# A two-layer decoder trunk on one core: table transfers with 64 rows outermost, ring slots by use, taps tile by tile

## The chip, the cores and the metric

The kernel runs on one core of a Trainium2 chip. Five engines take part, each with its own instruction stream: TensorE (PE, matmuls; PEld is its loading of weights), VectorE (DVE), ScalarE (ACT), GpSimd (POOL) and SyncE (SP), which here issues every transfer between the chip's main memory (DRAM) and the core's working memory (SBUF), one after the other. The transfers themselves are carried out by 16 DMA engines of the core. The metric is the device time of one execution in microseconds (us); the median of three runs is compared.

## The reference

The input x is 1024 tokens by 1024 channels, all float32. Two layers follow each other, each with an RMSNorm before and after its mixer and a residual.

```python
# layer 0: dilated attention, 16 heads of 64, three groups (window, dilation) = (128,1), (512,4), (2048,16)
proj = h @ w_in                                   # 1024 x (9*1024 + 1024): q, k, v of three groups, and a gate z
for g: o_g, lse_g = dilated_group_attention(q_g, k_g, v_g, rel_bias, window, dilation)
o = sum_g softmax_g(lse)[g] * o_g
x = x + rms_norm((o * silu(z)) @ w_out)
# layer 1: 64 groups of 16 channels, 64 complex states each
u, z = split(h @ w_in)                            # 1024 x 2048
a_bar = exp(A*dt); b_bar = (a_bar - 1)/A * B
states = scan over tokens of  s <- a_bar*s + b_bar u
y = real(C states) + d*u
g = gelu(y); y = g * sigmoid(g @ w_glu + b_glu)
x = x + rms_norm((y * silu(z)) @ w_out)
```

## The kernel before

Every large product is made as three products of a high and a low part (hi*hi, hi*lo, lo*hi), so each weight tile of 128 channels is loaded as float32 (`wraw`, L95, two buffers), cast by ACT to its high part (`whi`, L83), and the remainder is taken by DVE or POOL (`wlo`, L84). One such tile takes 48 matmuls of 128x512, 24 for each half of the tokens (`psj`, L110).

The program runs in this order. First the **value phase** (`v_phase`, up to about 390 us): the values of attention are computed chunk by chunk with a seven-product scheme (`Quads.values` and `Quads.quad`, matmuls L394 into `psq`). Each chunk loads its raw weights (`v<-in_w_v_dram`, L381) and stores its results to DRAM (`v_dr`, L400). Between these products the tables that layer 1 needs are built for its eight tiles `et` of eight groups each (`Prep.powers` and `Prep.products`): DVE forms `ca` (powers of the state's decay times C) and `zr`, `zi` (the same with B); `ca` goes to DRAM as `ca_dr` (L1208, two transfers a tile); PE forms the convolution taps from `ca` and `bd` (`pk`, L1223), which go through `Ks` to `k_dr` (L1228); PE turns `z` (`ptb`, L1235), which goes through `BT` to `bt_dr` (L1237).

Then comes **attention**, eight pairs of heads by three groups (about 390 to 1290 us). POOL makes one table of rotations per pair and group (`rt`, L1280 to L1285), which is stored as `rot_dr` (L1288, 24 transfers). The output of a pair goes to `on_dr`, and merging weights are read back as `mw`. The output product of layer 0 (`pso`, L865 to L867) runs until about 1390 us.

**Layer 1** (`layer1`, about 1390 to 1665 us) multiplies sixteen weight tiles, eight for u and eight for z. I call them w0 to w15 in order of use; w0 and w1 are loaded during the output product of layer 0. Between them run the stages of each tile `et`: `ssm_loads` reads the tables back (`BT`, `Cg` and `Sg` from `rot_dr`, `CA`, and the taps `M`), `ssm_input` reads the tile's u (`U`, L1333, which was stored by `u_dr`, L1400), `ssm_states` runs `pv` (L1348) and the scan on DVE, and `ssm_outputs` runs `py` (L1375) and stores y. The stages of tiles 0 and 1 are loaded ahead of everything. After that come the gated product (`glu`) and the output.

Small staging tiles come from a ring with two tags, "a" with three buffers and "b" with four. `Ctx.slot` gives the tags in turn unless a tag is named. A framework (a tile scheduler) orders the instructions on each engine: within the program's dependences it places them by a simulated timeline and by priorities, and the loads of weights have a high priority. What is written earlier in the program is therefore not always issued earlier, and a change of one transfer can move others. Each engine then runs its list strictly in order. SP is such a list too: a transfer that SP can't hand over holds all that stand behind it.

Of the kernel before, what the change touches and what calls it, by code (L numbers as in the profile page):

```python
# [15 lines left out]
F32 = mybir.dt.float32  # L16
# [7 lines left out]
P = 128  # L24
S = 1024
# [20 lines left out]
HEADS = (slice(0, 64), slice(64, 128))  # L46
# [218 lines left out]
class Quads:  # L265
# [47 lines left out]
    def quad(self, raw, order, product, banks, use):  # L313
# [3 lines left out]
        c, nc = self.c, self.c.nc  # L317
        b11, b12, b21, b22 = raw
        n = b11.shape[2]
# [27 lines left out]
        for i in order:  # L347
# [8 lines left out]
            with c.tc.high_priority(AHEAD):  # L356
                for b, ps in enumerate(acc):
# [3 lines left out]
                    elif i == 1:  # L361
                        t = c.slot("c11")
# [774 lines left out]
class Prep:  # L1137
# [60 lines left out]
    def powers(self, et):  # L1198


        c, nc = self.c, self.c.nc
# [4 lines left out]
        for n in range(2):  # L1206
            dst = bass.AP(c.ca_dr.tensor, c.ca_dr.offset + (et * 2 + n) * 64 * 1152, [[144, 2], [1152, 64], [288, 4], [1, 144]])
            nc.sync.dma_start(dst, ca[n])  # L1208
        z = outers(c, [c.slot("zr"), c.slot("zi")], self.tmp, [y[:, ps] for y in self.bp], [raw[:, n, :, 0] for n in range(2)])
# [5 lines left out]
    def products(self, et):  # L1215
# [8 lines left out]
        Ks = c.slot("Ks")[0:32].rearrange("p (k x) -> p k x", k=4)  # L1224
# [5 lines left out]
        for b in range(2):  # L1230
            BT = c.slot("BT").rearrange("p (g r s) -> p r g s", g=4, r=2)
# [28 lines left out]
def rotations(c, et, part):  # L1260
# [26 lines left out]
    dst = bass.AP(c.rot_dr.tensor, c.rot_dr.offset + (et * 3 + part) * 64 * S, [[P, 2], [S, 64], [256, 4], [1, P]])  # L1287
    nc.sync.dma_start(dst, out.rearrange("p (k x) -> p k x", k=4))  # L1288
# [14 lines left out]
def ssm_loads(self):  # L1303
# [9 lines left out]
    if et % 4 == 0:  # L1313

        c.taps = c.pb.tile([P, 4, 8, P], F32, tag=("b1", "b3")[et // 4], name="taps")
        koff = c.k_dr.offset + et * 8 * 16 * 240
        for m in range(8):
            src = bass.AP(c.k_dr.tensor, koff + 16 * m, [[240, 16], [16 * 240, 32], [1, 128]])
            nc.sync.dma_start(c.taps[16 * m:16 * m + 16].rearrange("p e g x -> p (e g) x"), src)
    self.M = c.taps[:, et % 4]  # L1320
    dr = c.rot_dr
    nc.sync.dma_start(self.BT, c.bt_dr[et].rearrange("p (g x) -> p g x", g=8))
    nc.sync.dma_start(self.Cg.rearrange("p g x -> p (g x)"),
                      bass.AP(dr.tensor, dr.offset + et * 3 * 64 * S, [[0, 2], [S, 64], [1, S]]))
    nc.sync.dma_start(self.Sg.rearrange("p g x -> p (g x)"),
                      bass.AP(dr.tensor, dr.offset + (et * 3 + 1) * 64 * S, [[S, P], [1, S]]))
    nc.sync.dma_start(self.CA, c.ca_dr[et].rearrange("p (g x) -> p g x", g=8))

# [62 lines left out]
def layer1(c, a, h1, ws):  # L1391
# [17 lines left out]
    groups = [Ssm(c, a, e) for e in range(8)]  # L1409
    at = [[] for _ in range(40)]  # L1410
# [209 lines left out]
```

## Time and profile before

| | |
|---|---|
| three runs, median | 1868.26 us (1868.19 to 1870.78) |
| the profiled execution, its own time | 1870.87 us |
| its span, first to last instruction | 1869.1 us |
| PE busy | 1707.9 us (91%) |
| DVE, ACT, POOL busy | 1045.7, 798.3, 461.7 us |
| mean granted PE clock | 0.963 |
| moved by the DMA engines | 212.67 MB, 114 GB/s mean |

Times in a row are microseconds from the start of the span unless they are marked ns. A row of the timeline gives start, duration, engine, line of the source, operation, output<-input with shapes, how often, and in brackets the idle time of that engine just before, with what ended it. SPq rows are the transfers that SP issues; a duration well above a third of a microsecond there means that SP was held while it handed the transfer over. A row of the windows gives a stretch, its length, the busy time of each engine in it with the number of instructions, the granted PE clock, the mean busy share of the 16 DMA engines and the GB/s that they moved. A row of the waits gives who waited, for whom, us in total, times, longest.

### The profile page before, as it was taken

How to read it: one execution, taken by the hardware profiler on the slowest of the kernel's cores; microseconds unless marked ns; L12 is line 12 of the kernel's file. 1: busy time of each engine (PE TensorE's matmuls, PEld its weight loads, DVE VectorE, ACT ScalarE, POOL GpSimd, SP SyncE). 2: the span in 40 equal slices, each digit the busy share in tenths (PEclk: the TensorE clock that was granted, in tenths of full speed). 3: DMA queues.
4: the chain of work that ended last, by engine and by line, in shares of the span. 5: the costliest groups of instructions: out<-in, count | busy, mean ns of one | idle time of the engine just before them, and what ended most of it. 6: DMA issues, size and time to landing. Idle time of an engine off the chain costs nothing. (4 is left out here: it accounts for less than half of the span.)

```text
span 1869.1 us, 25668 instructions
## 1 busy us (share of the span) xinstructions
PE 1707.9 (91%) x9262; PEld 1436.9 (77%) x9262; DVE 1045.7 (56%) x2565; ACT 798.3 (43%) x1912; POOL 461.7 (25%) x314
## 2 busy tenths in 40 slices
PE   7999978899979989899999999998995499989998
PEld 5889867787868778687787888876885488877886
DVE  7788766624544545455454555557461278764532
ACT  5222221235645656456465656564351122233411
POOL 2000000031242232322425142314220044432221
PEclk9999989899989999899999999998998799999999
DMA  6223342351231222313223232417257756646432
GB/s 237 70 67 104 113 139 88 116 161 50 72 93 47 74 78 82 84 57 98 68 74 105 75 106 82 127 58 198 91 126 154 179 187 216 197 130 192 146 119 90
DMA packets 174691, 212.67 MB, mean 114 GB/s; under 512 B 35153, under 2 KB 131172, under 8 KB 174564
## 3 DMA queue, kind: packets, MB, share of 16 engines
q1 hardware_dynamic: 174564, 211.03, 38.4%
q8 instruction: 73, 1.20, 0.3%
q14 instruction: 54, 0.44, 0.1%
HBM read 154.03 MB, written 56.96 MB: 113 GB/s over the span
## 5 line engine op out<-in xcount | busy, mean ns | idle before, releaser
L110 PE MATMUL psj<-hh,whi 128*128 128x512 f32 x896 | 363.9, 406 | 15.8 <-DVE ql L201 6.6
L110 PE MATMUL psj<-hl,whi 128*128 128x512 f32 x896 | 362.2, 404 | 0.0
L110 PE MATMUL psj<-hh,wlo 128*128 128x512 f32 x896 | 360.9, 403 | 0.0
L84 POOL TENSOR_TENSOR wlo<-wraw,whi 128x1024 fp32r<-128x1024 f32 x48 | 115.3, 2401 | 427.1 <-ACT whi L83 414.5
L110 PEld LDWEIGHTS psj<-hh,whi 128*128 128x128 f32 x896 | 172.2, 192 | 53.3 <-ACT kh L214 8.1
L110 PEld LDWEIGHTS psj<-hh,wlo 128*128 128x128 f32 x896 | 171.9, 192 | 35.9 <-issue 0.3
L110 PEld LDWEIGHTS psj<-hl,whi 128*128 128x128 f32 x896 | 172.4, 192 | 34.6 <-issue 0.7
L509 ACT ACTIVATE lg<-lg,nm 128x128 f32<-128x128 f32 (+1 forms) x384 | 168.2, 440 | 34.0 <-DVE nm L504 33.4
L498 DVE CUSTOM_DVE_ANT_0 lg<-psl,T 128x128 f32<-128x128 f32 (+1 forms) x384 | 116.7, 347 | 98.1 <-PE psl L495 97.0
L110 PE MATMUL psj<-h1h,whi 128*128 128x512 f32 (+1 forms) x272 | 108.8, 400 | 49.9 <-ACT whi L83 27.9
L83 ACT CAST whi<-wraw 128x1024 fp32r<-128x1024 f32 x80 | 83.6, 1045 | 165.5 <-PE psj L110 94.2
L394 PE MATMUL psq<-whi,v 128*128 128x256 f32 x640 | 122.1, 287 | 5.4 <-DVE v L366 5.4
L84 DVE TENSOR_TENSOR kl<-psj,kh 64x512 fp32r<-64x512 f32 x96 | 66.0, 687 | 86.6 <-ACT kh L83 85.3
L394 PEld LDWEIGHTS psq<-whi,v 128*128 128x128 f32 x640 | 101.8, 192 | 7.1 <-DVE v L366 6.1
L110 PE MATMUL psj<-h1l,whi 128*128 128x512 f32 (+1 forms) x272 | 107.0, 393 | 0.2 <-DVE h1l L84 0.2
L110 PE MATMUL psj<-h1h,wlo 128*128 128x512 f32 (+1 forms) x272 | 105.9, 391 | 0.0
L84 DVE TENSOR_TENSOR ph<-pt,ph 128x512 fp32r<-128x512 f32 (+1 forms) x128 | 78.8, 620 | 42.3 <-ACT ph L83 40.8
L110 PEld LDWEIGHTS psj<-h1h,whi 128*128 128x128 f32 x272 | 53.0, 195 | 62.4 <-ACT whi L83 28.4
L394 PE MATMUL psq<-wlo,v 128*128 128x256 f32 x320 | 91.8, 288 | 3.0 <-DVE wlo L84 3.0
L84 DVE TENSOR_TENSOR wlo<-wraw,whi 128x1024 fp32r<-128x1024 f32 x32 | 40.0, 1253 | 95.3 <-ACT whi L83 94.2
L83 ACT CAST whi<-v 128x1024 fp32r<-128x1024 f32 x35 | 36.8, 1051 | 128.1 <-PE psq L394 101.2
L1227 POOL TENSOR_TENSOR Ks<-Ks,O 32x64 f32<-32x64 f32 x8 | 3.8, 478 | 337.4 <-ACT Ks L1225 320.1
(292 smaller groups left out, 4055.2 us busy)
## 6 DMA issues: line engine op xcount, KB each, us to landing
wraw<-in_w_in_dram SPq DMA_DIRECT2D x56, 512.0 KB
mw<-wt_dr SPq DMA_DIRECT2D x48, 256.0 KB
v<-in_w_v_dram SPq DMA_DIRECT2D x20, 512.0 KB
vp<-v_dr SPq DMA_DIRECT2D x16, 512.0 KB
wraw<-in_ssm_w_in_dram SPq DMA_DIRECT2D x16, 512.0 KB
v_dr<-v SPq DMA_DIRECT2D x30, 256.0 KB
rot_dr<-rt SPq DMA_DIRECT2D x24, 256.0 KB
ca_dr<-ca SPq DMA_DIRECT2D x16, 288.0 KB
```

The source lines that it names most:

```text
L83: nc.scalar.copy(hi, src)
L84: return (engine or nc.vector).tensor_tensor(lo, src, f32(hi), op=ALU.subtract)
L110: nc.tensor.matmul(ps, a[:, s], b[:, k, :], start=first and k == 0 and n == 0, stop=k == KT - 1 and n == 2, skip_group_check=True)
L394: nc.tensor.matmul(o, r[x][:, k, ts], w[y][:, k, :], skip_group_check=True, start=i in (0, 4, 5) and t % 2 == k == n == 0, stop=k == 3 and ...
L498: nc.vector.tensor_tensor_reduce(lg[:, h, j, 0:w], ps[:, h, 0:w], bt[:, h, 256 - w:256], scale=1.0, scalar=-3.0e38, op0=ALU.add, op1=ALU.m ...
L509: nc.scalar.activation(lg[:, h, j, 0:w], lg[:, h, j, 0:w], AF.Exp, bias=nm[:, h, b:b + 1], accum_out=ms[:, col:col + 1])
L1227: nc.gpsimd.tensor_tensor(Ks[:, :, 0:16], Ks[:, :, 0:16], self.dd, op=ALU.add)
```

## The change

Three things are edited.

1. **Transfers.** A table of 128 partitions holds two halves of 64 rows that belong to even and odd groups. Before, one transfer covered both, and its DRAM side had a dimension of size 2 outermost (`[144, 2], [1152, 64], ...`). Now each half is a transfer of its own, with the 64 rows outermost. This is done to `ca_dr` (16 transfers become 32), to `rot_dr` (24 become 48), and to `Cg` (8 become 16), whose source had an outermost repeat of 2 with step 0.
2. **Ring slots.** In the value phase the stagings `c11` and `Ks` always take tag "a"; `zr`, `zi` and `BT` always take tag "b".
3. **Taps.** They were loaded by `ssm_loads` for four tiles at a time, 8 transfers of 256 KB each for tiles 0 and 4. Now a stage `ssm_taps` of its own loads them tile by tile, 8 transfers of 64 KB each, and stands one step after `ssm_loads` in the program; the 16 transfers become 64, with the same bytes. The loads of tile 1 also come one step after those of tile 0, no longer with them.

```diff
-                        t = c.slot("c11")
+                        t = c.slot("c11", tag="a")
...
         for n in range(2):
-            dst = bass.AP(c.ca_dr.tensor, c.ca_dr.offset + (et * 2 + n) * 64 * 1152, [[144, 2], [1152, 64], [288, 4], [1, 144]])
-            nc.sync.dma_start(dst, ca[n])
-        z = outers(c, [c.slot("zr"), c.slot("zi")], self.tmp, [y[:, ps] for y in self.bp], [raw[:, n, :, 0] for n in range(2)])
+            for s in range(2):
+                dst = bass.AP(c.ca_dr.tensor, c.ca_dr.offset + (et * 2 + n) * 64 * 1152 + s * 144, [[1152, 64], [288, 4], [1, 144]])
+                nc.sync.dma_start(dst, ca[n][HEADS[s]])
+        z = outers(c, [c.slot(x, tag="b") for x in ("zr", "zi")], self.tmp, [y[:, ps] for y in self.bp], [raw[:, n, :, 0] for n in range(2)])
...
-        Ks = c.slot("Ks")[0:32].rearrange("p (k x) -> p k x", k=4)
+        Ks = c.slot("Ks", tag="a")[0:32].rearrange("p (k x) -> p k x", k=4)
...
-            BT = c.slot("BT").rearrange("p (g r s) -> p r g s", g=4, r=2)
+            BT = c.slot("BT", tag="b").rearrange("p (g r s) -> p r g s", g=4, r=2)
...
-    dst = bass.AP(c.rot_dr.tensor, c.rot_dr.offset + (et * 3 + part) * 64 * S, [[P, 2], [S, 64], [256, 4], [1, P]])
-    nc.sync.dma_start(dst, out.rearrange("p (k x) -> p k x", k=4))
+    for s in range(2):
+        dst = bass.AP(c.rot_dr.tensor, c.rot_dr.offset + (et * 3 + part) * 64 * S + s * P, [[S, 64], [256, 4], [1, P]])
+        nc.sync.dma_start(dst, out[HEADS[s]].rearrange("p (k x) -> p k x", k=4))
...
-    if et % 4 == 0:
-        c.taps = c.pb.tile([P, 4, 8, P], F32, tag=("b1", "b3")[et // 4], name="taps")
-        koff = c.k_dr.offset + et * 8 * 16 * 240
-        for m in range(8):
-            src = bass.AP(c.k_dr.tensor, koff + 16 * m, [[240, 16], [16 * 240, 32], [1, 128]])
-            nc.sync.dma_start(c.taps[16 * m:16 * m + 16].rearrange("p e g x -> p (e g) x"), src)
-    self.M = c.taps[:, et % 4]
...
-    nc.sync.dma_start(self.Cg.rearrange("p g x -> p (g x)"),
-                      bass.AP(dr.tensor, dr.offset + et * 3 * 64 * S, [[0, 2], [S, 64], [1, S]]))
+    for hf in HEADS:
+        nc.sync.dma_start(self.Cg[hf].rearrange("p g x -> p (g x)"),
+                          bass.AP(dr.tensor, dr.offset + et * 3 * 64 * S, [[S, 64], [1, S]]))
...
+def ssm_taps(self):
+    c, et = self.c, self.et
+    if et % 4 == 0:
+        c.taps.append(c.pb.tile([P, 4, 8, P], F32, tag=("b1", "b3")[et // 4], name="taps"))
+    t = self.M = c.taps[et // 4][:, et % 4]
+    for m in range(8):
+        src = bass.AP(c.k_dr.tensor, c.k_dr.offset + et * 8 * 16 * 240 + 16 * m, [[240, 16], [16 * 240, 8], [1, 128]])
+        c.nc.sync.dma_start(t[16 * m:16 * m + 16], src)
...
-        for stage, d in ((ssm_loads, 3 if e > 1 else -1 - t), (ssm_input, 5), (ssm_states, 7), (ssm_outputs, 10)):
+        for stage, d in ((ssm_loads, (-1, -2)[e] if e < 2 else 3), (ssm_taps, 4), (ssm_input, 5), (ssm_states, 7), (ssm_outputs, 10)):
             at[t + d + 1].append((stage, e))
```

The framework makes new lists from this. Three places show what moved. The first is SP at the start of layer 1, up to the load of w2 (`wraw`; `xr` is the last residual tile of layer 0, `BT`, `Cg`, `Sg`, `CA` are the tables of tile 0 and then of tile 1). Before:

```order
L932 DMA xr<-in_x_dram 128x1024
L1319 DMA taps<-k_dr 16x32x128 x8
L1322 DMA BT<-bt_dr 128x1024
L1323 DMA Cg<-rot_dr 128x1x1024
L95 DMA wraw<-in_ssm_w_in_dram 128x1024
```

After:

```order
L1333 DMA taps<-k_dr 16x8x128
L1316 DMA BT<-bt_dr 128x1024
L932 DMA xr<-in_x_dram 128x1024
L1318 DMA Cg<-rot_dr 64x1024 x2
L1320 DMA Sg<-rot_dr 128x1024
L1322 DMA CA<-ca_dr 128x1152
L1316 DMA BT<-bt_dr 128x1024
L1318 DMA Cg<-rot_dr 64x1024 x2
L95 DMA wraw<-in_ssm_w_in_dram 128x1024
```

Ahead of w2, eight taps transfers of 256 KB have become one piece of 64 KB; the tables of tile 0 and most of those of tile 1 now stand ahead of it, and so does `xr` behind two of them.

The second place is the same list up to the load of w3 (the last `wraw` of the first fence, the first of the second fence; behind it there come w4 and w5). Before:

```order
L1327 DMA CA<-ca_dr 128x1152
L1319 DMA taps<-k_dr 16x32x128 x6
L1400 DMA u_dr<-ut 128x4x128
L1319 DMA taps<-k_dr 16x32x128 x2
L943 DMA post<-in_ssm_post_norm_dram 128x1024
L95 DMA wraw<-in_ssm_w_in_dram 128x1024
```

After:

```order
L1406 DMA u_dr<-ut 128x4x128
L973 DMA x_dr<-xr 128x1024
L1333 DMA taps<-k_dr 16x8x128 x5
L1406 DMA u_dr<-ut 128x4x128
L1333 DMA taps<-k_dr 16x8x128 x15
L95 DMA wraw<-in_ssm_w_in_dram 128x1024
L1333 DMA taps<-k_dr 16x8x128 x10
L1406 DMA u_dr<-ut 128x4x128 x2
L95 DMA wraw<-in_ssm_w_in_dram 128x1024
L1333 DMA taps<-k_dr 16x8x128 x3
L95 DMA wraw<-in_ssm_w_in_dram 128x1024
L1339 DMA U<-u_dr 128x1024 x2
```

Between w2 and w3 there stood, before, the rest of the tables, a `u_dr`, an `x_dr`, all eight taps transfers of tiles 4 to 7, another `u_dr` and `post`. Now there stand `Sg` and `CA` of tile 1, 24 taps pieces (4 of them ahead of the rows shown), two `u_dr` and `x_dr`. Thirteen more pieces stand between w3 and `U`, with two `u_dr`, w4 and w5.

The third place is PE a little later, where the first state product `pv` of tile 0 stands (`psj` with the numbers 13147 before and 13183, 13211 after are products of weight tiles; `whi_13137` before and `whi_13179` after are w3; `whi_13241` and `whi_13291` are w4). Before:

```order
L110 MATMUL psj_13169<-h1h1_12541,whi_13137 128x512
L110 MATMUL psj_13169<-h1l1_12542,whi_13137 128x512
L110 MATMUL psj_13169<-h1h1_12541,wlo_13138 128x512
L1348 MATMUL pv_13200<-U_13133,BT_12886 128x128 x4
L1348 MATMUL pv_13221<-U_13133,BT_12886 128x128 x4
L110 MATMUL psj_13245<-h1h0_12087,whi_13241 128x512
```

After:

```order
L110 MATMUL psj_13183<-h1l0_12128,whi_13179 128x512
L110 MATMUL psj_13183<-h1h0_12127,wlo_13180 128x512
L1354 MATMUL pv_13242<-U_13175,BT_12926 128x128
L110 MATMUL psj_13211<-h1h1_12581,whi_13179 128x512
L110 MATMUL psj_13211<-h1l1_12582,whi_13179 128x512
```

Before, `pv` stood behind both halves of w3. Now its first matmul stands between the two halves of w3, so PE needs `U` of tile 0 half a weight tile earlier.

More of the change, by code (lines that the diff above doesn't have):

```diff
@@ L1409, in layer1 @@
     groups = [Ssm(c, a, e) for e in range(8)]
+    c.taps = []
     at = [[] for _ in range(40)]
```

## The prediction

> **What bounds the kernel now.** PE is busy for 91% of the span, so only time in which PE stands or runs slowly can be won. I read PE's own waits first, the longest on top:
>
> ```profile
> PE psj L110 <- ACT whi L83: 28.1, 2, 27.9
> ...
> PE psj L110 <- ACT ut L1398: 14.5, 1, 14.5
> ```
>
> One stall of 27.9 us and one of 14.5, both on a cast of a weight tile or a copy queued behind it. Then the windows, to see which stages lose anything:
>
> ```profile
> 190.00:390.00 200.00, 165.34 (x1267) 157.56 (x1266) 127.62 (x193) 45.46 (x75) 10.80 (x17) 0.92 0.39 122
> ...
> 1480.00:1560.00 80.00, 80.00 (x428) 67.81 (x427) 57.74 (x80) 22.45 (x35) 33.12 (x32) 1.00 0.58 182
> ```
>
> The second half of the value phase leaves PE idle for 34.7 of 200 us; layer 1, once under way (1480 to 1560), leaves nothing at full clock. So a saving ahead of 1480 is not eaten by a limit behind it: the rest of layer 1 is PE's own work. Third, the timeline around the two long stalls:
>
> ```profile
> 1390.57 10.53 SPq L1319 DMA_DIRECT2D taps<-k_dr  x8
> ...
> 1390.85 0.39 PE L110 MATMUL psj<-h1l,whi 128*128 128x512 f32 x1
> 1391.08 0.40 PE L110 MATMUL psj<-h1h,wlo 128*128 128x512 f32 x1
> ...
> 1404.11 4.12 SPq L95 DMA_DIRECT2D wraw<-in_ssm_w_in_dram  x1
> ...
> 1417.93 11.12 SPq L1325 DMA_DIRECT2D Sg<-rot_dr  x1
> ...
> 1428.51 1.04 ACT L83 CAST whi<-wraw 128x1024 fp32r<-128x1024 f32 x1 [18.75 <-DMA wraw<-in_ssm_w_in_dram]
> 1430.10 0.80 PE L110 MATMUL psj<-h1h,whi 128*128 128x512 f32 x1 [14.52 <-ACT ut L1398]
> 1430.69 0.63 PE L110 MATMUL psj<-h1l,whi 128*128 128x512 f32 x1
> 1431.11 0.63 PE L110 MATMUL psj<-h1h,whi 128*128 128x512 f32 x1
> ...
> 1436.52 17.75 SPq L1319 DMA_DIRECT2D taps<-k_dr  x6
> 1462.22 0.38 SPq L95 DMA_DIRECT2D wraw<-in_ssm_w_in_dram  x1
> 1471.91 0.79 PE L110 MATMUL psj<-h1h,whi 128*128 128x512 f32 x1 [27.92 <-ACT whi L83]
> ```
>
> PE ran out of work at 1415.6 (1430.10 less 14.52) because w2 landed only at 1428.5, and again 27.9 us before 1471.9 because SP did not hand over w3 before 1462.2. SP was held in between: 11.12 us for one `Sg`, which stands behind a `Cg`, and 17.75 us for six taps transfers. The matmuls after a stall also come 0.42 us apart instead of 0.23 (1430.69 to 1431.11 against 1390.85 to 1391.08). Thirteen such pitches come to about 2.5 us, an estimate of what each long stall costs on top. This place therefore loses 14.5 + 27.9 + 2 x 2.5 = 47.4 us.
>
> In the value phase the same view of waits, for 180 to 400 us alone, names everything:
>
> ```profile
> PE psq L394 <- ACT c L363: 10.7, 1, 10.7
> PE ptb L1235 <- ACT BT L1236: 6.3, 1, 6.3
> PE ptb L1235 <- ACT Ks L1225: 5.7, 1, 5.7
> PE psq L394 <- DVE v L366: 5.4, 2, 3.0
> PE psq L394 <- DVE wlo L84: 3.6, 3, 1.6
> PE psq L394 <- ACT v L360: 2.6, 1, 2.6
> ```
>
> The engines named are not slow; they stand on transfers themselves:
>
> ```profile
> 246.99 7.75 SPq L400 DMA_DIRECT2D v_dr<-v  x1
> ...
> 263.43 1.05 ACT L83 CAST whi<-v 128x1024 fp32r<-128x1024 f32 x1 [11.77 <-DMA v<-in_w_v_dram]
> ...
> 290.15 6.11 SPq L1208 DMA_DIRECT2D ca_dr<-ca  x2
> 296.35 8.17 SPq L1237 DMA_DIRECT2D bt_dr<-BT  x1
> ...
> 309.23 0.59 ACT L363 COPY c<-psq 128x512 f32<-128x512 f32 x1 [9.49 <-DMA bt_dr<-BT]
> ...
> 319.67 7.71 SPq L400 DMA_DIRECT2D v_dr<-c  x1
> ...
> 360.77 0.76 DVE L1251 TENSOR_TENSOR ca<-O,O 128x576 f32<-128x576 f32 x1 [5.28 <-DMA ca_dr<-ca]
> ```
>
> Each of the three SP holds of 7.7 to 8.2 us comes right behind a `ca_dr` (the rows at 290 and 296; the other two alike). The `c` copy at 309 wants a ring slot that the held `bt_dr` occupies: here the ring and the transfers meet. How wide a `ca_dr` runs is seen where little else moves, and how fast the same engines can go shortly after:
>
> ```profile
> 290.00:300.00 10.00, 10.00 (x82) 9.34 (x81) 9.88 (x18) 1.43 (x2) 0.00 (x0) 1.00 0.13 33
> ...
> 380.00:390.00 10.00, 10.00 (x76) 9.52 (x75) 2.07 (x3) 2.85 (x4) 3.72 (x2) 1.00 0.91 300
> ```
>
> A share of 0.13 is 2 of 16 engines, at 33 GB/s; with 0.91 of them busy they moved 300. The Trainium skill, page "DMA: Bandwidth & Descriptors", section "Why a DMA increments its semaphore by 16 and not by 1", says that a transfer uses the largest number up to 16 of engines that divides the outermost sizes of both sides; the row agrees, with 2 outermost before and 64 or 256 now.
>
> **The change part by part.** *Value phase.* `ca_dr` as halves over all engines: 288 KB at 300 GB/s is 1 us; if its short rows went no faster than the 122 GB/s of the whole phase, 2.4 us. Either is well below the 6 to 8 us for which it held SP. Of PE's 34.3 us of waits in the list, all but `wlo` (3.6) hang on these holds: 30.7. The three longest also cost slow matmuls behind them, some 5 us together. The most that can come back is 36. Not all will: DVE has 127.6 us of work here, 77% of a phase shortened to 165, and one chunk's weights still land late if DVE frees them late. I take 30. The low bound is 12, if only the two stalls that end on a ring slot (`Ks` 5.7, `BT` 6.3) go. The fixed tags add no instruction. Sixteen more issues on SP cost 0.33 us each at the least (row below), hidden on a queue that now has slack; without that cover, 5 us.
>
> *Start of layer 1.* I add up the transfer queue as the new list has it, from 1390.6, where PE frees the space (first row of the third fence). Prices:
>
> ```profile
> L1319 SPq DMA_DIRECT2D taps<-k_dr x16: 326/1680/5779, 1390.6 to 1457.7; - x16
> ```
>
> ```profile
> 526.88 0.64 SPq L633 DMA_DIRECT2D cm<-ms_dr  x1
> ...
> 529.21 0.18 DVE L636 TENSOR_TENSOR cm<-cm 64x32 f32<-64x32 f32 x1 [6.78 <-DMA cm<-ms_dr]
> ```
>
> A 512 KB table or weight tile takes 1.75 us at 300 GB/s, `CA` 1.97. A taps transfer took 1.32 us (10.53 for eight) to 2.96 (17.75 for six), so a quarter of one takes 0.33 to 0.74; I take 0.57. A `u_dr`, rows of the same 512 bytes and 256 KB, is 4 x 0.57 = 2.3. Landing comes 2.3 us behind (526.88 to 529.21).
>
> - Ahead of w2: one piece, six tables, `xr`, counted with w2 itself 0.57 + 7 x 1.75 + 1.97 = 14.8. It lands at 1390.6 + 14.8 + 2.3 = 1407.7, ahead of PE's need at 1415.6. This stall goes. `xr` now waits behind a piece and a `BT`, 0 to 2.3 us; I charge 1.
> - From w2 to w3: `Sg`, `CA`, 24 pieces, two `u_dr`, `x_dr`, w3: 1.75 + 1.97 + 13.7 + 4.6 + 1.75 + 1.75 = 25.5. It lands at 1433.2 and is cast at 1434.3. PE, with 48 matmuls at 0.23 (11.2 us) for w2, wants it at 1427.8: a stall of 6.5, with 1.5 of slow matmuls.
> - From w3 to `U` of tile 0: 13 pieces, two `u_dr`, w4, w5, `U`: 7.4 + 4.6 + 5.3 = 17.3, landing at 1450.5. PE reaches the moved `pv` after half of w3, at 1434.3 + 5.6 + 1.5 = 1441.4: a **new stall** of 9, plus 2 of slow matmuls. Behind it on PE stands the rest of w3, and everything after.
>
> The rest of the taps (26 pieces, 15 us) goes by under w4 and w5, 22 us of matmuls. So 20 us stay of 47.4, and 27 come back. With pieces at 0.33 (and a `u_dr` at 1.3) about 41 come back, at 0.74 about 18.
>
> The skill's rule against the split is in the same page, section "Rules for kernel authors": transfers of 64 KB and less are mostly overhead, to be joined. The row's minimum of 0.33 us of SP for each of 48 more is 16 us; this is inside my piece price, not added to it.
>
> *Attention.* `rot_dr` held others too:
>
> ```profile
> 895.35 0.54 SPq L1288 DMA_DIRECT2D rot_dr<-rt  x1
> 897.72 3.05 SPq L717 DMA_DIRECT2D on_dr<-O  x1
> 905.30 1.18 ACT L582 COPY O<-pso 64x512 f32<-64x512 f32 x2 [9.78 <-DMA on_dr<-O]
> ```
>
> ```profile
> PE pso L572 <- DVE O L583: 4.4, 1, 4.4
> ```
>
> That one stall (4.4) goes; the other waits of this stage follow no `rot_dr` closely. I take 4, between 0 and 8. The second half of each `rot_dr` is an SP issue more, hidden under PE work (48 transfers in 800 us).
>
> Sum: 30 + 27 + 4 = 61. From the profiled execution's 1870.9 that is 1810; the median of the runs lies 2.6 lower, so **1807**.
>
> **The rivals.** A, *the value phase turns to DVE*: queue free, but PE then waits for DVE's table work or for a chunk's weights. For: DVE's 64% with two of the six waits on it. Against: its longest own wait is itself a transfer. Half the gain, 15: 1822. B, *the small pieces are dear*: at 1 us a piece w3 lands 10.3 later and `U` 16 later; stalls become 17 and 15, with `xr` and the slow matmuls 36 of 47 stay: 30 + 11 + 4 = 45 won, 1823. C, *the pieces are cheap*, 0.33 (the row's minimum), the value phase gives 36, layer 1 41 and attention 8: 85 won, 1783. D, the slower side, *a transfer has a price of its own whatever it carries*: a piece takes the median 1.68 and half a `ca_dr` as long as half of the 6.11 that two held, 3.05. Then w3 lands 27 later and `U` 42 later than summed, 62 us are lost instead of 47 (layer 1 turns to a loss above 1.3 a piece), and sixteen more `ca_dr` add 49 us of queue, of which half shows: 1868 + 15 + 24 = 1907. Against it: eight whole taps went out at 1.32 each, and SP's holds grow with what lies in the queue. E, *the halves win nothing*, because each pair keeps the same engines for as long: `Cg` still holds for 11 us each, w2 lands near 1426, the three stalls are 12, 13 and 9 with 7 of slow matmuls and `xr`, the value phase stays: 6 won, 1862. The skill's "Rules for kernel authors" say this of transfers to the two halves of the partitions, that they serialize and aren't worth splitting. Against it stands the share of 0.13: the whole transfer did not use the engines.
>
> **How the numbers follow.** Forecast 0.62, A 0.13, B 0.10, C 0.07, D 0.04, E 0.04. The range 1782 to 1838 holds the forecast with its bounds, C, A and B, and leaves out D and E. Within 0.2% (3.7 us), which is about what the runs can tell from no change, lies only part of E. So faster 0.94, same 0.02, slower 0.04.
>
> **What would show it.** Right: no PE wait above 4 us between 190 and 390 and a `ca_dr` that holds SP for under 2 us; w2 cast before 1415 on the old clock; shorter stalls ahead of w3 and ahead of the first `pv`, the latter ended by `U`; from there PE full. It would be wrong if the value phase shows new PE waits on DVE, if taps rows on SP stay near 1.7 us each, or if 290 to 300 has its like with a share of 0.13.

## The result, and the profile after

The changed kernel takes 1781.16 us (median of 4 runs, 1780.57 to 1784.87) against 1868.22 before (4 runs beside them, 1865.20 to 1870.78). The ratio is 0.954, 95% interval 0.952 to 0.956. The forecast was 1807 with a range from 1782 to 1838: the direction is right, 26 us more were won than forecast, and the median stands 0.8 us under the low end of the range. The profiled execution spans 1778.9 us instead of 1869.1, so there are 90.2 us to place.

The windows view, first of the kernel before and then of the changed one, cut at the same four places of the program: the value phase (first to last matmul of L394), attention, the output product of layer 0 (from the first L865), and layer 1 from the first taps transfer to its last `py`. Columns as in the prediction: the stretch, its length, busy time of PE, PEld, DVE, ACT, POOL, granted clock, DMA share, GB/s.

```profile
113.50:387.50 274.00, 238.91 (x1880) 229.41 (x1879) 190.85 (x409) 62.70 (x96) 9.47 (x16) 0.94 0.36 114
387.50:1289.50 902.00, 856.99 (x4522) 707.57 (x4521) 459.61 (x1352) 523.41 (x1443) 281.62 (x160) 0.98 0.30 86
1289.50:1390.50 101.00, 97.24 (x433) 78.59 (x432) 60.71 (x195) 43.16 (x100) 32.72 (x18) 0.97 0.38 116
1390.50:1674.50 284.00, 233.65 (x1219) 197.01 (x1217) 159.06 (x248) 67.87 (x110) 80.93 (x78) 0.91 0.65 174
```

```profile
113.50:345.50 232.00, 228.63 (x1880) 220.03 (x1879) 191.02 (x410) 62.21 (x96) 10.23 (x16) 1.00 0.43 133
345.50:1243.50 898.00, 855.56 (x4522) 707.37 (x4521) 461.37 (x1350) 525.87 (x1444) 284.54 (x161) 0.98 0.31 88
1243.50:1340.50 97.00, 95.39 (x435) 77.19 (x434) 59.88 (x199) 42.87 (x99) 30.58 (x18) 1.00 0.35 111
1340.50:1584.00 243.50, 230.34 (x1216) 193.97 (x1215) 161.82 (x245) 67.54 (x109) 82.45 (x78) 0.98 0.67 203
```

The same work stands in each stretch (the counts agree within a few). The value phase is 42.0 us shorter, attention 4.0, the output of layer 0 4.0, layer 1 40.5. The length less PE's busy time is PE's idle time: in the value phase it falls from 35.1 to 3.4, and PE's busy time falls as well, from 238.9 to 228.6, since fewer matmuls run slowly (granted clock 0.94 before, 1.00 now). In layer 1 idle time falls from 50.4 to 13.2 and busy time by 3.3.

The value phase from 190 us on, in the changed kernel, and the only wait of PE in it that is over half a microsecond:

```profile
190.00:355.00 165.00, 161.77 (x1296) 153.39 (x1295) 129.85 (x196) 46.00 (x77) 16.06 (x19) 1.00 0.51 153
```

```profile
PE psq L394 <- DVE wlo L84: 2.6, 2, 1.8
```

DVE now carries 129.85 us of work in 165 and is late only in these two places. At the start of layer 1 the timeline of the changed kernel reads:

```profile
1340.40 0.33 SPq L1333 DMA_DIRECT2D taps<-k_dr  x1
...
1344.50 1.97 SPq L1318 DMA_DIRECT2D Cg<-rot_dr  x2
1346.57 0.53 SPq L95 DMA_DIRECT2D wraw<-in_ssm_w_in_dram  x1
...
1363.27 8.22 SPq L1333 DMA_DIRECT2D taps<-k_dr  x15
1364.75 1.05 ACT L83 CAST whi<-wraw 128x1024 fp32r<-128x1024 f32 x1 [4.34 <-PE psj L110]
...
1371.59 0.38 SPq L95 DMA_DIRECT2D wraw<-in_ssm_w_in_dram  x1
...
1376.03 1.05 ACT L83 CAST whi<-wraw 128x1024 fp32r<-128x1024 f32 x1 [9.18 <-DMA wraw<-in_ssm_w_in_dram]
...
1381.44 0.85 SPq L1339 DMA_DIRECT2D U<-u_dr  x2
...
1387.89 0.77 PE L1354 MATMUL pv<-U,BT 128*128 128x128 f32 x2 [4.09 <-DMA U<-u_dr]
```

SP hands w2 over 6.2 us after the first taps piece; its cast waits for PE, not for the transfer. w3 lands just in time: ACT waits for it, PE does not. The one stall left at this place is the 4.09 us ahead of the moved `pv`, ended by `U`. (Three waits on `z` further on, 7.9 us in all, are as in the kernel before, where they come to 7.5.) The 15 taps pieces of one row take 8.22 / 15 = 0.55 us each; this includes the short waits of SP between them.

So far this looks like the forecast with larger sizes. The experiments show that one of its terms, attention, is right only by accident, and that a term it put at nothing, the fixed tags, costs 28 us.

### The profile page after: what moved, and what is told of

It is laid out like the page before. It is cut to its first block, busy times and chain, and to the rows that moved or that the text cites. A ratio compares the mean times of both kernels' runs of the same rounds, so it can differ in the third digit from the quotient of the medians.

```text
span 1778.9 us, 25782 instructions
## 1 busy us (share of the span) xinstructions
PE 1691.9 (95%) x9262; PEld 1423.9 (80%) x9262; DVE 1052.6 (59%) x2565; ACT 799.8 (45%) x1912; POOL 464.8 (26%) x314
## 5 line engine op out<-in xcount | busy, mean ns | idle before, releaser
L110 PE MATMUL psj<-hh,whi 128*128 128x512 f32 x896 | 365.8, 408 | 15.6 <-ACT kh L214 6.3
L110 PE MATMUL psj<-hl,whi 128*128 128x512 f32 x896 | 361.6, 404 | 0.0
L110 PE MATMUL psj<-hh,wlo 128*128 128x512 f32 x896 | 361.3, 403 | 0.3 <-POOL wlo L84 0.3
L110 PEld LDWEIGHTS psj<-hh,whi 128*128 128x128 f32 x896 | 173.0, 193 | 52.7 <-ACT kh L214 7.9
L110 PEld LDWEIGHTS psj<-hh,wlo 128*128 128x128 f32 x896 | 172.1, 192 | 37.0 <-POOL wlo L84 0.7
L110 PEld LDWEIGHTS psj<-hl,whi 128*128 128x128 f32 x896 | 172.6, 193 | 34.2 <-issue 0.2
L394 PE MATMUL psq<-whi,v 128*128 128x256 f32 x640 | 118.7, 283 | 0.0
L110 PE MATMUL psj<-h1h,whi 128*128 128x512 f32 (+1 forms) x272 | 107.0, 394 | 8.8 <-DVE z L1412 7.9
L110 PE MATMUL psj<-h1l,whi 128*128 128x512 f32 (+1 forms) x272 | 105.3, 387 | 0.2 <-DVE h1l L84 0.2
L110 PE MATMUL psj<-h1h,wlo 128*128 128x512 f32 (+1 forms) x272 | 105.2, 388 | 0.0
L84 DVE TENSOR_TENSOR ph<-pt,ph 128x512 fp32r<-128x512 f32 (+1 forms) x128 | 78.2, 620 | 44.1 <-ACT ph L83 42.8
L394 PEld LDWEIGHTS psq<-whi,v 128*128 128x128 f32 x640 | 99.6, 189 | 1.0 <-ACT whi L83 0.6
L394 PE MATMUL psq<-wlo,v 128*128 128x256 f32 x320 | 90.7, 284 | 1.8 <-DVE wlo L84 1.8
L83 ACT CAST kh<-psj 64x512 fp32r<-64x512 f32 x96 | 55.8, 581 | 59.5 <-PE psl L495 50.4
L83 ACT CAST ph<-pt 128x512 fp32r<-128x512 f32 (+1 forms) x128 | 66.2, 532 | 34.5 <-PE pt L520 29.7
```

The source lines that it names most:

```text
L83: nc.scalar.copy(hi, src)
L84: return (engine or nc.vector).tensor_tensor(lo, src, f32(hi), op=ALU.subtract)
L110: nc.tensor.matmul(ps, a[:, s], b[:, k, :], start=first and k == 0 and n == 0, stop=k == KT - 1 and n == 2, skip_group_check=True)
L394: nc.tensor.matmul(o, r[x][:, k, ts], w[y][:, k, :], skip_group_check=True, start=i in (0, 4, 5) and t % 2 == k == n == 0, stop=k == 3 and ...
```

## The experiments

The theory going in (W): a transfer whose outermost dimension is 2 runs on 2 of the 16 engines and holds SP and whatever stands behind it; making it wide is what wins, in the value phase and ahead of w2 and w3. Its rivals: it was the ring slots that stalled the value phase (R); it was the amount of taps ahead of w2 and w3 that stalled layer 1 (O); it is the number and size of the transfers that counts, not their width (N).

### The three parts one at a time

Transfers alone, the kernel before with (and likewise `rot_dr`, `Cg`):

```diff
-            dst = bass.AP(..., [[144, 2], [1152, 64], [288, 4], [1, 144]])
-            nc.sync.dma_start(dst, ca[n])
+            for s in range(2):
+                dst = bass.AP(..., [[1152, 64], [288, 4], [1, 144]])
+                nc.sync.dma_start(dst, ca[n][HEADS[s]])
```

> The kernel before with only the transfers changed: ca_dr, rot_dr and Cg go as two transfers with 64 rows outermost; ring slots and taps stay as before. Theory W (width: a transfer with 2 outermost keeps 2 of the 16 engines and holds SP behind it): the value phase gives about 38 us (the last L394 lands near 349 instead of 387), attention 4; at the start of layer 1 all 8 whole taps still stand ahead of w2 and 8 more ahead of w3, so the 14.5 us stall on w2 goes, but of the 27.9 on w3 some 11 to 25 stay: 22 us won. Total about 1804. Theory R (ring: the value phase stalled because c11, z, BT and Ks shared ring slots): the value phase gives under 10, total about 1834. Theory E (two halves keep the same engines as one whole): no change, 1862 to 1868.

Ring tags alone, the kernel before with:

```diff
-                        t = c.slot("c11")
+                        t = c.slot("c11", tag="a")
...
-        z = outers(c, [c.slot("zr"), c.slot("zi")], ...)
+        z = outers(c, [c.slot(x, tag="b") for x in ("zr", "zi")], ...)
...
-        Ks = c.slot("Ks")...
+        Ks = c.slot("Ks", tag="a")...
-            BT = c.slot("BT")...
+            BT = c.slot("BT", tag="b")...
```

> The kernel before with only the ring tags fixed (c11 and Ks on a, zr, zi and BT on b). Theory W: SP is still held by ca_dr, so at most the two stalls that end on a ring slot (Ks 5.7, BT 6.3) shrink, and most of that comes back as a later wait: 0 to 10 us won, 1863. Theory R: the value phase gives most of its 42 us, about 30: 1838.

Taps alone, the kernel before with `ssm_taps` as in the change, and:

```diff
-        for stage, d in ((ssm_loads, 3 if e > 1 else -1 - t), (ssm_input, 5), ...
+        for stage, d in ((ssm_loads, (-1, -2)[e] if e < 2 else 3), (ssm_taps, 4), (ssm_input, 5), ...
```

> The kernel before with only the taps loaded tile by tile in a stage of their own (64 pieces of 64 KB in place of 16 of 256 KB; the two first tables a stage apart). Theory W: two whole Cg of 11 us each still stand ahead of w2, which now stands behind both, so its stall stays at about 12; w3 comes about 10 late instead of 27.9 and the first pv waits about 9 for U: 11 us won, 1857. Theory O (order: what counts at the start of layer 1 is how much of the taps stands ahead of w2 and w3, not how wide Cg runs): nearly all of the layer-1 gain, 27 to 40: 1828 to 1841. The value phase does not change in either.

And the changed kernel with its taps part undone (the last diff reversed):

> The changed kernel with its taps part undone: transfers in halves and fixed ring tags, but 16 whole taps transfers of 256 KB, all ahead of w3. Theory W with the taps as a cause of their own: value phase and attention as in the changed kernel, the w3 stall of 11 to 25 us back, U without a stall: 1795 to 1805. If the taps part is worth nothing once Cg is wide: 1781. If it brought all of the 40 us at layer 1: 1821. The difference to the run with the transfers alone is what the ring tags are worth when SP is free: 0 to 4 us by W, 30 by R.

Measured, against 1866.43 before beside them: transfers alone **1773.87** (ratio 0.951, 0.948 to 0.954), tags alone **1909.53** (1.022, 1.020 to 1.025), taps alone **1841.89** (0.987, 0.984 to 0.990), transfers with tags **1803.75** (0.966, 0.964 to 0.969). The transfers alone come out 7 us below the whole change (the intervals of the two ratios overlap), and the tags alone make the kernel slower. None of my theories had either: W said 1804 for the transfers and 1863 for the tags, R 1834 and 1838. The taps alone were said to give 1857 by W and 1828 to 1841 by O; that run is next to O. Transfers with tags came out as foretold (1795 to 1805). By stages, in us, worked out from the starts of the same instructions in the timeline of one execution each (first and last L394, first L865, first taps transfer, last `py`; the run without tags follows below):

| stage | before | transfers | tags | taps | transfers + tags | transfers + taps | whole change |
|---|---|---|---|---|---|---|---|
| value phase | 273.7 | 229.4 | 272.6 | 272.4 | 231.2 | 229.9 | 231.7 |
| attention | 902.2 | 869.8 | 945.3 | 903.2 | 895.3 | 871.0 | 898.3 |
| output of layer 0 | 101.1 | 100.1 | 96.7 | 94.9 | 96.5 | 94.9 | 96.7 |
| layer 1 to the last `py` | 283.8 | 263.4 | 284.5 | 260.7 | 271.1 | 244.5 | 243.5 |

The value phase answers R: the tags alone give 1.1 us, the transfers alone 44.3. There was no ring problem apart from the held queue. Layer 1 answers O: the transfers give 20, the taps give 23 by themselves, and together 39: both were in the way, about half each. They act at different stalls. In the run with the transfers alone the stall on w2 falls from 14.5 to 5.4 us and that on w3 only from 27.9 to 18.7 (first fence); in the run with the taps alone that on w3 is gone and that on w2 is as long as before (second fence). The taps part also moves the loads of tile 1 two steps of the program (not one) behind those of tile 0; what this does by itself no run shows.

```profile
PE psj L110 <- ACT whi L83: 18.9, 2, 18.7
...
PE psj L110 <- ACT ut L1401: 5.4, 1, 5.4
```

```profile
PE psj L110 <- ACT ut L1401: 16.6, 2, 14.8
```

And attention shows two large effects that cancel in the change: -32 by the transfers, +43 by the tags alone, or +25 to +27 on top of the transfers. The windows view of that stretch, of the run with the transfers alone, and then of the run with the tags alone:

```profile
343.00:1213.00 870.00, 843.25 (x4525) 698.91 (x4524) 459.60 (x1351) 524.05 (x1444) 284.19 (x160) 0.99 0.32 89
```

```profile
386.00:1331.50 945.50, 876.52 (x4524) 718.85 (x4524) 460.43 (x1351) 526.86 (x1447) 285.45 (x161) 0.95 0.29 85
```

Beside the row of before (902.00, 856.99): the transfers take 18 us of idle time and 14 us of PE's busy time out of attention, for the same matmuls; the tags put 24 and 20 in. Both had to be explained.

### Why `rot_dr` was worth 32 us in attention

The kernel before with `rot_dr` alone in halves:

```diff
-    dst = bass.AP(c.rot_dr.tensor, ..., [[P, 2], [S, 64], [256, 4], [1, P]])
-    nc.sync.dma_start(dst, out.rearrange("p (k x) -> p k x", k=4))
+    for s in range(2):
+        dst = bass.AP(c.rot_dr.tensor, ... + s * P, [[S, 64], [256, 4], [1, P]])
+        nc.sync.dma_start(dst, out[HEADS[s]].rearrange("p (k x) -> p k x", k=4))
```

> The kernel before with only rot_dr in halves (64 rows outermost). The run with all transfers in halves showed the attention 32 us shorter in the same written order, where I had summed 4. Theory W2: all of it is rot_dr, which runs on 2 of 16 engines for several us 24 times and holds on_dr, mw and weights behind it: attention 870, 1836. Rival: rot_dr is worth the one stall on O (4) and the rest came from somewhere else, such as a steadier clock after the value phase: 1860 to 1864.

Measured: **1838.16** (ratio 0.986, 0.982 to 0.990; 23.6 us below the 1861.76 of before beside it). In the profiled executions attention falls from 902.2 to 872.0, by 30.2 us, layer 1 by 3.1, and the value phase is unchanged (274.0), so that a steadier clock behind it is no cause. The rows that I had missed, in the timeline of the kernel before (the second is `ms_dr`, a store of 16 KB with the rows' maxima and sums, right behind a `rot_dr`; `cm` reads it back):

```profile
518.19 0.56 SPq L1288 DMA_DIRECT2D rot_dr<-rt  x1
518.85 4.67 SPq L617 DMA_DIRECT2D ms_dr<-mt  x1
526.88 0.64 SPq L633 DMA_DIRECT2D cm<-ms_dr  x1
```

and in the kernel with `rot_dr` in halves:

```profile
517.53 0.52 SPq L1289 DMA_DIRECT2D rot_dr<-rt  x1
518.48 0.33 SPq L617 DMA_DIRECT2D ms_dr<-mt  x1
518.86 1.79 SPq L1289 DMA_DIRECT2D rot_dr<-rt  x1
521.67 0.60 SPq L633 DMA_DIRECT2D cm<-ms_dr  x1
...
523.97 0.18 DVE L636 TENSOR_TENSOR cm<-cm 64x32 f32<-64x32 f32 x1 [2.19 <-DMA cm<-ms_dr]
```

The store is held 4.67 us instead of 0.33, `cm` is read 8.0 us after its store began instead of 3.2, and DVE, which runs in order, stands on it for 6.78 us (the row at 529.21 in the prediction) instead of 2.19. This happens once for each pair of heads. From the start of the store to that of the read it takes 8.0, 5.0, 7.3, 3.3, 3.6, 2.1, 1.4 and 2.0 us in the kernel before, and 3.2, 1.5, 2.0, 1.4, 1.5, 1.4, 1.4 and 2.0 with the halves; in seven of the eight a `rot_dr` stands 0.7 to 8.5 us ahead of the store, and the closer it stands, the longer it takes on the whole. The sum falls by 18.2 us, and the waits of DVE for `cm` by as much. Those waits, before and then with the halves, attention alone:

```profile
DVE cm L636 <- DMA cm<-ms_dr: 26.5, 8, 6.8
```

```profile
DVE cm L636 <- DMA cm<-ms_dr: 8.8, 6, 3.4
```

PE's waits for DVE's `ms` fall with it from 16.2 to 6.6 us, those for `ql` from 6.6 to 2.1, and the stall on `O` (4.4) goes. That is 18.5 us; smaller waits give 2.3, and PE's busy time, for the same matmuls, falls by 9.4.

### What the ring tags did

The tags add and remove nothing, but the planner works with a simulated timeline, and it wrote another order. The traces list 4520 PE instructions in attention (the expectations below count 4409). Lined up by names and shapes, the kernels with all four tags hold 2610 to 2626 of them in the sequence of those without, which agree with each other in all 4520. Only PE's order was compared. Theory S: this order is worse on the chip. Two rivals: the small taps had made up for it (K), or the ring itself is crowded (S2, S3). Four runs, each the changed kernel with some of the four tags undone: all of them; all but `c11`, `zr`, `zi`, `BT`; all but `zr`, `zi`, `BT`, `Ks`; all but `Ks`. For the first,

```diff
-                        t = c.slot("c11", tag="a")
+                        t = c.slot("c11")
-        z = outers(c, [c.slot(x, tag="b") for x in ("zr", "zi")], ...)
+        z = outers(c, [c.slot("zr"), c.slot("zi")], ...)
-        Ks = c.slot("Ks", tag="a")...
+        Ks = c.slot("Ks")...
-            BT = c.slot("BT", tag="b")...
+            BT = c.slot("BT")...
```

and for the others one or three of these pairs: only the `Ks` pair, only the `c11` pair, and all but the `Ks` pair.

> The changed kernel with only the ring tags undone (c11, zr, zi, Ks and BT alternate again); transfers in halves and taps tile by tile stay. New theory S, from the runs with the transfers alone (1774) and the tags alone (1910): the fixed tags make the planner write another order for the whole of the attention (of its 4409 matmuls only about 2550 stand in the same order), and this order is some 28 us longer on the chip. Without the tags the attention takes 870 us instead of 898, the value phase 229 to 232, layer 1 from the first taps to the last py 243: 1752. Rival K: the tags cost only together with whole taps, the small taps had already cured it: 1781.

> The changed kernel with three of the four ring tags (c11 on a, zr and zi and BT on b), Ks alternating as before. In this form the order that the planner writes for the attention is that of the kernel before, but for 6 instructions. Theory S (it is the order): attention 870, 1752 to 1756. Rival S2 (it is the ring itself: slot b with four buffers is crowded by z and BT, so that transfers and copies wait for slots): about 1781.

> The changed kernel with three of the four ring tags, another three than before: zr and zi and BT on b and Ks on a, c11 alternating. Here the planner writes for the attention, matmul by matmul, the order of the changed kernel. Theory S (the order costs): attention 898, 1777 to 1785, though this has as many fixed tags as the run with c11, z and BT (1763). Rival S2 (c11 is the tag that costs): 1753 to 1763.

> The changed kernel with one ring tag only, Ks on a. The order of the attention that the planner writes here has all but 2 of 4409 matmuls as in the kernel before. Theory S: attention 870 to 877, 1753 to 1763. Rival S3 (Ks on slot a, which has three buffers, is what holds the attention up, since it is what the run at 1763 left out): attention 898, about 1781.

| fixed tags (beside transfers and taps) | attention's written order | attention, us | time, us | ratio to before |
|---|---|---|---|---|
| none | as before | 871.0 | 1753.44 | 0.942 (0.937 to 0.947) |
| `Ks` | as before but 2 | 871.0 | 1752.99 | 0.938 (0.936 to 0.940) |
| `c11`, `zr`, `zi`, `BT` | as before but 6 | 877.3 | 1762.97 | 0.946 (0.942 to 0.950) |
| `zr`, `zi`, `BT`, `Ks` | as the whole change | 897.8 | 1778.08 | 0.952 (0.949 to 0.954) |
| all four | the whole change | 898.3 | 1781.16 | 0.954 (0.952 to 0.956) |

Attention's time follows the order and not the number or kind of tags: in all runs with wide transfers it takes 870 to 877 us in the order of before and 895 to 898 in that of the whole change. `Ks` costs nothing alone, and whether it or `c11` joins `zr`, `zi` and `BT` decides which order is written. This rules out K, S3 and `c11` as the costly tag, and S2 as the cause of the 27 us. From the orders the first run was foretold at 1752, that with `Ks` at 1753 to 1763 and that with `zr`, `zi`, `BT` and `Ks` at 1777 to 1785, and so they came out; the one with `c11`, `zr`, `zi` and `BT` was foretold at 1752 to 1756 and is 7 us above that. The profiled execution of the run with `c11`, `zr`, `zi` and `BT` is 13 us longer than that of the one without tags (the medians differ by 10): 6.3 lie in attention and 6.3 in the output of layer 0. The first I can't place, so a small cost of these tags beside the order is not ruled out; for the second see the last experiment. The times of this table come from runs beside different runs of before (1861.76 to 1869.99). By the ratios the four tags cost 22 us against none and 30 against `Ks` alone; by the medians it is 28 both times.

What is worse in that order can be seen at one place. First the changed kernel, then the one without tags, around the step that merges a pair's output (L707 waits for the merging weights `mw`; `ql` is a low part that DVE takes from a projection's result, and the next projection waits for it):

```profile
922.59 1.22 DVE L707 TENSOR_TENSOR O<-O,mw 128x1024 f32<-128x1024 f32 x1 [5.67 <-DMA mw<-wt_dr]
...
924.19 0.69 DVE L201 SCALAR_TENSOR_TENSOR ql<-psj,ql 64x512 fp32r<-64x512 f32 x1
...
925.03 0.76 PE L110 MATMUL psj<-hh,whi 128*128 128x512 f32 x1 [2.94 <-DVE ql L201]
```

```profile
906.71 0.69 DVE L201 SCALAR_TENSOR_TENSOR ql<-psj,ql 64x512 fp32r<-64x512 f32 x1
...
913.67 1.23 DVE L707 TENSOR_TENSOR O<-O,mw 128x1024 f32<-128x1024 f32 x1 [2.63 <-DMA mw<-wt_dr]
```

With the tags `ql` stands behind the merge, whose transfer is late, and PE waits for it; without them it stands 7 us ahead. Counting matmuls of L110 in both timelines, the changed kernel is about 3 us behind at 810 us, 10 at 860, 11 at 900 and 23 at 950; the rest of the 27 comes in small steps. So some 20 us arise in two stretches, each with a merge in it. Three or four waits of PE stand in each (5.3 and 7.6 us together, where the kernel without tags has 0.7); the 2.94 on `ql` is the longest, and the others I have not followed back.

### Width, or number and size

The kernel without tags, with `ca_dr` and `Cg` cut by columns instead of rows: more and smaller transfers, all still with 2 outermost.

```diff
-            for s in range(2):
-                dst = bass.AP(..., + s * 144, [[1152, 64], [288, 4], [1, 144]])
-                nc.sync.dma_start(dst, ca[n][HEADS[s]])
+            for k in range(4):
+                dst = bass.AP(..., + k * 288, [[144, 2], [1152, 64], [1, 144]])
+                nc.sync.dma_start(dst, ca[n][:, k])
...
-    for hf in HEADS:
-        nc.sync.dma_start(self.Cg[hf]..., bass.AP(..., [[S, 64], [1, S]]))
+    for s in range(2):
+        nc.sync.dma_start(self.Cg...[:, s * H:s * H + H], bass.AP(..., [[0, 2], [S, 64], [1, H]]))
```

> The changed kernel without ring tags, with the ca_dr and Cg transfers cut another way: ca_dr into four by columns, Cg into two by columns, each still with 2 outermost, so that there are as many or more transfers and they are smaller, but no wider. rot_dr stays in halves by rows. Theory W (width): the value phase loses its gain again (about 40 us longer than with rows, PE waits on BT, Ks, c) and Cg holds SP ahead of w2 and w3 (12 us): 1795 to 1808, and a share of 0.13 where only ca_dr moves. Rival N (it is the number and size of transfers that frees SP's queue): 1752 to 1760.

Measured: **1808.41**, 55 us above the same kernel with rows and at the upper end of what W gave; the value phase 267.0 instead of 229.9, layer 1 259.3 instead of 244.5. The long waits of PE are back, though not all the same ones: `c` takes 10.2 us (10.7 before) and `wlo` 11.2 (3.6 before), but `BT` and `Ks`, which I had also expected, don't return. A piece of `Cg` holds SP for up to 8.3 us:

```profile
PE psj L110 <- ACT ut L1404: 14.6, 2, 11.7
...
PE psq L394 <- DVE wlo L84: 11.2, 4, 4.4
PE psq L394 <- ACT c L363: 10.2, 1, 10.2
```

```profile
L1318 SPq DMA_DIRECT2D Cg<-rot_dr x16: 493/511/8331, 1352.3 to 1550.2; - x16
```

The transfers by themselves, in a kernel that leaves all the computation out:

> Leaves the whole computation out (the output is zeros): it only measures groups of transfers by themselves, each group of four tiles of data, a memset on DVE between groups, the list gone through twice. Theory W (width): four whole ca_dr (1.15 MB, 2 outermost) run at a share of 0.13 and 33 GB/s and take 35 us, the four cut into sixteen by columns the same 35, eight halves by rows 4 to 10, four with 128 outermost the same 4 to 10; four whole rot_dr (1 MB) 30, halves 4 to 9; four whole Cg (2 MB) about 45 at the 11 us that one held SP, halves 7 like four plain tables. Rival N (number and size): columns go as fast as rows, and halves are no faster than whole. Taps: eight of 256 KB and 32 of 64 KB both carry 2 MB; by my price of 0.57 a piece 18 us against 10.5 for eight whole, by the minimum of 0.33 equal.

From a memset on DVE that starts a group to the one that ends it, read as the latter's idle time (two passes), and how long SP took to hand the group over (first pass; the row of its transfers in the timeline):

| group | pieces | first, second pass, us | SP, us |
|---|---|---|---|
| `ca_dr` whole, 2 outermost | 4 of 288 KB | 33.9, 33.8 | 21.8 |
| `ca_dr` halves by rows, 64 outermost | 8 of 144 KB | 7.8, 7.4 | 5.3 |
| `ca_dr` by columns, 2 outermost | 16 of 72 KB | 33.7, 33.4 | 27.1 |
| same rows of 576 bytes, 128 outermost | 4 of 288 KB | 5.9, 6.0 | 2.8 |
| `rot_dr` whole | 4 of 256 KB | 26.7, 26.7 | 17.4 |
| `rot_dr` halves | 8 of 128 KB | 7.5, 7.1 | 5.2 |
| `Cg` whole | 4 of 512 KB | 42.5, 42.8 | 12.8 |
| `Cg` halves | 8 of 256 KB | 11.4, 12.1 | 5.2 |
| plain table | 4 of 512 KB | 8.4, 8.6 | 1.8 |
| taps whole | 8 of 256 KB | 23.5, 22.9 | 9.5 |
| taps pieces | 32 of 64 KB | 17.9, 17.7 | 15.0 |

Four of these stretches in the windows view (only DVE and POOL are listed as engines, both idle; then clock, DMA share and GB/s): `ca_dr` whole, halves, columns, and 128 outermost; and below them the taps, whole and in pieces.

```profile
22.00:52.00 30.00, 0.00 (x0) 0.00 (x0) 1.00 0.14 37
56.00:62.00 6.00, 0.00 (x0) 0.00 (x0) 1.00 0.84 196
65.00:95.00 30.00, 0.00 (x0) 0.00 (x0) 1.00 0.14 38
98.00:102.00 4.00, 0.00 (x0) 0.00 (x0) 1.00 0.92 277
...
204.00:223.00 19.00, 0.00 (x0) 0.00 (x0) 1.00 1.21 95
228.00:241.00 13.00, 0.00 (x0) 0.00 (x0) 1.00 0.69 132
```

Cutting by columns changes nothing, 0.14 of the engines and 38 GB/s either way; cutting by rows takes the share to 0.84. N falls in both runs; rival E of the prediction fell with the transfers alone. This agrees with the rule cited in the prediction (the Trainium skill, page "DMA: Bandwidth & Descriptors", section "Why a DMA increments its semaphore by 16 and not by 1"), by which 2 outermost give 2 engines: 2/16 is 0.125 beside the 0.14. The same page of the Trainium skill, section "Rules for kernel authors", advises against two transfers to the two partition halves, on the ground that both halves use the same engines anyway, and for one transfer of 128 partitions. Here the one transfer did not use all the engines, and the measurement (33.9 against 7.8 us) decides for the split. Where the layout allows 128 outermost in one transfer, that is better still (5.9).

### The stall that was left

One more run takes the kernel without tags and places tile 0's first `pv` and `py` on PE behind the last matmul of w3 (`py` is edited in the same way).

```diff
+        with c.tc.issue_after(c.last_proj) if et == 0 else ExitStack():
             for j in range(4):
                 nc.tensor.matmul(pv[:, j, :], ...)
```

> The changed kernel without ring tags, and with the first pv and py of tile 0 placed behind the last matmul of w3 on PE instead of after half of it. Theory: the stall of 3.9 us ahead of the first pv goes with its slow matmuls (1 to 2), since U lands about when w3 is through: 1747 to 1750 against 1753 without this. Rival: the wait only moves, DVE is late with the first scan and the first py stalls PE instead: 1753 to 1758.

Measured: **1752.34** (ratio 0.937, 0.933 to 0.940), beside 1753.44 (0.942) without it: no difference that these runs can tell, and above the 1747 to 1750 foretold. The wait on `U` is gone and layer 1 is 239.4 instead of 244.5, as foretold, but the output of layer 0 is 100.3 instead of 94.9 and attention 874.7 instead of 871.0. The written order of the PE instructions of attention is the same here. The output of layer 0 goes with one wait of PE, that of L865 on `gh`: the wait is 3.5 to 3.8 us in the six runs in which the stage takes 100 to 101, 2.9 in the run with `Ks` (98.0), 1.2 to 1.6 where it takes 96 to 97, and absent in the two that take 94.9. What makes `gh` late in one kernel and not in another is open.

## Why the prediction was right, and where it wasn't

**Value phase** (said 30, at most 36; measured 42.0). The mechanism holds: it was the narrow `ca_dr` that held SP, the cut by columns brings the loss back, and no PE wait above 2.6 us in all is left between 190 and 355. Mis-sized was the ceiling: I added "some 5 us" of slow matmuls for the three longest waits. The windows say that PE's busy time fell by 10.3 us; that the short waits had slow matmuls behind them too is my reading of the difference and was not measured wait by wait. And the deduction "not all will" for DVE was empty: nothing came back there (idle time fell by 31.7 of the 34.3 us of waits listed). Rival A is refuted. A `ca_dr` piece held SP for 0.52 us at the median, 2.1 at the most, as I had said of a right forecast.

**Fixed tags** ("add no instruction", costed at nothing). This is the step that failed. They cost 28 us, 27 of it in attention, in which they stage nothing. The written order of the changed kernel was there to be compared, and some 1900 of 4520 PE instructions of that stretch stood elsewhere in it; I read the order only at the three places that my sum spoke of.

**Attention** (said 4, between 0 and 8; measured 3.9). The number is right and its reason is not. "The other waits of this stage follow no `rot_dr` closely" is wrong: for seven of the eight pairs a `rot_dr` stood ahead of the small `ms_dr` on whose return DVE stands still, and PE behind DVE. It looked as if DVE were the cause since the list of PE's waits says "DVE ms"; one step further back, DVE's own wait says "DMA cm". The halves won 30 to 32, the tags lost 27; that the two came to the 4 of the forecast is luck.

**Start of layer 1** (said 27, between 18 and 41; measured 40.5, at the bound). The price of a piece was of the right size: 0.57 taken; 0.55 in the row shown above, 0.56 for a group by itself (17.9 / 32), though the 24 pieces from w2 to w3 come to 0.73 (17.45 in three rows, the waits of SP in them included). The way from w2 to w3 agrees in its total, 25.5 us in my sum against 25.0 from one handover to the other (1346.57 to 1371.59), but not in what makes it up: SP handed over for 13.0 of them, and for 12.1 it stood, mostly until `CA`, `BT`, `Sg` or `Cg` had landed. My sum had a queue that is always full, so this agreement is luck in part. Too high was the part ahead of w2, where I took seven transfers at 1.75 us and `CA` at 1.97: SP handed w2 over after 6.2 us, and w3 was cast at 35.6 us after the start, instead of 43.7 in my sum. The stall ahead of w3 (6.5) never came, and that on `U`, which I had foreseen with its place and its cause, was 4.1 instead of 9. The rule that I set against the split speaks, in the words of the Trainium skill (page "DMA: Bandwidth & Descriptors", section "Rules for kernel authors"), of transfers under 64 KB; the pieces have just 64, and here they were no dearer than whole taps (17.9 against 23.5 us). Also, the sum put the cause on the order and the `Cg` together without dividing it; the runs show 20 us for the transfers alone, 23 for the taps alone, and 39 for both.

**Output of layer 0** (not in the sum; measured 4.0 to 4.5). In the kernel before it has a 3.8 us wait on `gh` and in the changed one 1.6; why `gh` comes earlier is open, as above.

**The rivals.** C gave 1783 and is nearest in time, with 36 + 41 + 8, but not for its reasons: its premise, pieces at 0.33 us, is not borne out (0.55 and 0.73 above), and attention gave 4, the net of some 31 and 27, not 8. B falls with the piece at 0.55 to 0.73, and D with that and with the `ca_dr` piece at 0.52. E falls with the transfers alone.

## What to carry to other kernels

Look at the outermost size on both sides of every transfer, at a small one first of all when it holds a queue: 2 outermost took 3.5 to 4.6 times as long as two transfers with 64 outermost (the table of groups), and the price is paid by whatever stands behind on the issuing queue, at times a 16 KB store whose reader stalls another engine. Follow a wait back through two engines before it is put down to the one that the list names. Where a planner orders the code from a simulated timeline, an edit that adds no instruction can move work hundreds of microseconds away: compare the whole written order, stretch by stretch, and try each part of a change alone; here the change without its four ring tags takes 1753 us, 28 less than with them.

## What the runs showed of the hardware that was not expected

- The number of pieces did not matter for narrow transfers: 4 of 288 KB and 16 of 72 KB took 33.9 and 33.7 us.
- Small taps pieces were not only no dearer but faster: 32 of 64 KB in 17.9 us, 8 of 256 KB in 23.5, with the same rows of 512 bytes and the same 2 MB. The DMA share reads 1.21 for the large ones, above full, at 95 GB/s; what the engines did there is open.
- Two halves by rows take longer than one transfer with 128 outermost: 7.8 against 5.9 us for the same 1.15 MB.
- Where PE's idle time fell, its busy time for the same matmuls fell too: by 10.3 us in the value phase beside 31.7 us of idle time (before against the whole change), and by 13.7 in attention beside 18.3 (before against the transfers alone).
